# DeltaNet heads of a decoder layer, taken in pairs through one chain of steps instead of singly through two alternating chains

## The chip, the cores and the metric

One core of one Trainium2 chip runs the whole program. The metric is device time in microseconds (us), as the median of several runs; lower is better. The engines are named as the profile names them: PE is TensorE (matmuls), PEld its load of weights, DVE is VectorE, ACT is ScalarE, POOL is GpSimd, and SP issues most transfers.

## What is computed

One layer of a hybrid decoder, for a prompt of 512 tokens and for 8 sequences of 4 sample tokens, which share the weights. Width is 1024, all in float32. The layer is a half-step feed-forward, a token mixer, and a second half-step feed-forward. The mixer has one large input projection and two branches, whose gated outputs are added and projected again. Branch A is a gated DeltaNet with 8 heads of 128 by 128, branch B a sliding-window attention. Cut to the mixer and the delta rule:

```python
proj = h @ p['w_in']
u, z, b_raw, a_raw, q_sw, k_sw, v_sw, gate_a, gate_b = jnp.split(proj, split_idx, axis=-1)
u, conv_new = short_conv(u, conv_buf, p['conv_w'])
...
o_dn, S_new = gated_delta_rule(q_dn, k_dn, v_dn, g, beta, S0)
o_dn = rmsnorm(o_dn, p['dn_norm']) * jax.nn.silu(z)
...
y = jax.nn.sigmoid(gate_a) * o_dn + jax.nn.sigmoid(gate_b) * o_sw
return y @ p['w_out'], ...

def gated_delta_rule(q, k, v, g, beta, S0):
    # S_t = a_t (I - b_t k_t k_t^T) S_{t-1} + b_t k_t v_t^T,  o_t = S_t^T q_t
    ...
    lower = jnp.where(strict, einsum('bnhid,bnhjd->bnhij', kb, kc) * decay, 0.0)
    sol = triangular_solve(eye(C) + lower, rhs)
    ...
    def step(S, xs):
        v_new = un - wn @ S
        o = (qn * exp(gn)) @ S + an @ v_new
        S = S * exp(g_last) + k_dec.T @ v_new
        return S, o
```

For the prompt the kernel uses chunks of 128 tokens, so a head has 4 chunks (`NC`). For each it inverts a triangular 128 by 128 matrix; then the state S goes through the chunks one after the other.

## The kernel before

**Products.** Each float32 weight and activation is split into a high and a low part of the type fp32r (hi and lo of a weight; hh and hl of an activation), and a product is three matmuls: hi with hh, hi with hl, lo with hh. They are the matmuls of line L301, on 272 columns (half of the 544 tokens). The split of a weight is one pass on ACT (L270, hi) and one on DVE or POOL (L271, lo).

**The mixer's work, and who orders it.** The instructions' order is found on the host by `Streams` (L145 to L181). A main stream gives units of projections to TensorE in the order of `ORDER` (L49): the blocks B, U0 and U1 (the columns of q, k and v of heads 0 to 3), K, V and Q of the attention, then U2, G0, U3 and G1 to G7 (G is a gate block: a gate of the attention, z and a gate of the DeltaNet, one block for each head). Side streams (the DeltaNet chains, the attention, the sample tokens' DeltaNet, the merges) are generators. At each `yield` they give a cost, which moves a virtual clock on, and a delay, times `LATK`, after which they are due again; whenever a unit of the main stream has been put in, the streams that are due put in their next step. The side streams' steps thus stand between projections. When main has no more units ahead of a wait, the side streams' steps follow one another.

**The DeltaNet chains.** Two streams run `delta_stream` (`NSTR` = 2): one takes the heads 0, 2, 4, 6, the other 1, 3, 5, 7. Each takes one head at a time (`G` = 1), so the tiles of a chain hold M = G x NC = 4 matrices. The chain of a head, in `delta` and `inverse`:
- E from memory (L1249), the decays Dm (L1252 and the exps on ACT), transposes pkt of k (L1260) with squares on ACT, and the rsqrt rk: 11 small DVE instructions in a row (L340 to L345).
- pkq (L1281), NT and AT on DVE (L1285, L1287).
- `inverse`: the 32 by 32 diagonal blocks of NT go to memory and back (L1393, L1398), which puts the 16 by 16 blocks one to a partition. Then come 15 steps of two DVE instructions, a product pr (L1420) and a subtraction (L1422), then a way back through memory (L1427, L1430), and four levels of small matmuls (L1440, L1448 and L1451, L1464, L1474 and L1478, L1486, L1491), each with a copy or subtraction on ACT or DVE.
- transposes (L1301), kdec and vs (L1302) and the scaling of k and q (L1304) on DVE.
- the loop over the chunks: pks (L1317), R on DVE (L1319), pvn (L1325), vn on ACT (L1328), psu (L1333) and poT (L1339, L1341), the state S on DVE (L1344, in the first chunk the copy L1348), od and the square o2 on ACT (L1350, L1352), the sum tq on POOL (L1354).
- at the head's end pro (L1362), rx (L1364), the rsqrt ro, prb (L353, called at L1369), the product od on DVE (L1370), and the store of od to memory (L1372).

`merge_stream` loads a head's od again (L1540) when both od and the gate z (L1526) of that head are there, and merges them (L1547, L1549). At the mixer's end main waits for the merges of the heads 0 to 3, splits them into hh and hl, gives TensorE the first halves of two blocks of the output projection (w_out), then does the same for the heads 4 to 7 (L1909 to L1917). The chain's last results are therefore needed by the second halves of these two blocks and by all that follows.

Of the kernel before, what the change touches and what calls it, by code (L numbers as in the profile page):

```python
# [28 lines left out]
FF = 2752  # L29
NH = 8  # L30
NC = SEQ // P
G = 1
NSTR = 2
M = G * NC
EPS = 1e-6
NEG = -1e30
# [29 lines left out]
WD = 0  # L66
HP_S = 300
HP_E = 0
KQ_BUFS = 4
L_CVO = 2.0  # L70
L_B1 = 6.0
L_SUB = 3.5
# [715 lines left out]
class Mixer:  # L788
# [431 lines left out]
    def head_blocks(self, gi):  # L1220
# [3 lines left out]
        def tiles():  # L1224
            if not st:
                st["kq"] = self.kqp.tile([P, G, 2, SEQ], F32, tag="kq", name="kq")
                st["v"] = self.kqp.tile([P, G, SEQ], F32, tag="vT", name="vT")
            return st["kq"], st["v"]

        for n in range(G):  # L1230
            h = gi * G + n
            for kind, outs in ((1, lambda n=n, h=h: (tiles()[0][:, n, 0, :], self.kqs[:, h, 0, :])),
                               (0, lambda n=n, h=h: (tiles()[0][:, n, 1, :], self.kqs[:, h, 1, :])),
                               (2, lambda n=n, h=h: (tiles()[1][:, n, :], self.vts[:, h, :]))):
                use = self.conv_block(kind, h, outs)
                if n == G - 1 and kind == 2:
                    def use(ps, f=use):
                        f(ps)
                        self.kqv[gi] = tiles()
# [136 lines left out]
    def delta_stream(self, i, dp):  # L1376
        for gi in range(i, NH // G, NSTR):
            while gi not in self.kqv or not self.decays_done:
                yield 0.0, 1.0
            yield from self.delta(gi, *self.kqv[gi], dp, i)  # L1380
# [311 lines left out]
    def run(self, sch, feed):  # L1692
# [5 lines left out]
        c_ap, c_rp, c_tp, c_sp = ExitStack(), ExitStack(), ExitStack(), ExitStack()  # L1698
        self.kqp = L.pool("kqp", KQ_BUFS, ctx)
        self.cvp = L.pool("cvp", 1, ctx)  # L1700
        self.sc = {}
        self.conv_load(0)
        self.gp = L.pool("gp", 1, ctx)
        dps = [L.pool(f"dp{i}", 1, ctx) for i in range(NSTR)]
        self.ap = L.pool("ap", 1, c_ap)
# [46 lines left out]
    def plan(self, feed):  # L1752

        L, win, x = self.L, self.win, self.x
        self.att_done = [0] * 4
        self.kqv, self.z, self.gb_done = {}, [None] * NH, [False] * NH
        self.od_done, self.merged = [False] * NH, [False] * 10
        self.decays_done = False
        self.odd = L.dr.tile([NH, P, SEQ], F32, name="odd")
        qT, kT = (lambda: self.qT), (lambda: self.kT)  # L1760
        q = lambda c: [u for b in range(8) for u in L.project(win, Q0 + b * P, x, self.evac(qT, b, (c,)), cs=(c,),
                                                              pool_lo=False)]
        self.mark0 = feed.add(q(0))
        self.marks = []

        def ba(ps):
            self.sch.spawn(self.decays(ps, self.rp), 0)

        for n in ORDER:
            if n == "B":  # L1770
                us = L.project(win, BA0, x, ba, ncol=16)
            elif n == "Q":
                us = q(1)
            elif n == "K":
                us = [u for b in range(2) for u in L.project(win, K0 + b * P, x, self.evac(kT, b))]
            elif n == "V":
                us = [u for b in range(2) for u in L.project(win, V0 + b * P, x, self.v_block(b))]
            elif n[0] == "U":
                us = [u for h in (0, 1) for u in self.head_blocks(2 * int(n[1]) + h)]
            else:  # L1780
                us = self.gate_blocks(int(n[1]))
            self.marks.append((n, feed.add(us)))
# [186 lines left out]
```

## Time and profile before

| | |
|---|---|
| median of 3 runs | 1608.23 us (1606.12 to 1611.68) |
| the profiled execution | 1608.77 us |
| its span, first to last instruction | 1607.0 us |
| mean granted TensorE clock | 0.983 of full speed |
| the mixer's DeltaNet | about 550 to 1130 us of the span |
| busy: PE, DVE, ACT, POOL | 96%, 55%, 40%, 19% of the span |

The span is shorter than the execution's time by what lies around the first and the last instruction. The two levels of TensorE's clock are 1.2 and 2.4 GHz, so a granted clock of 0.90 in a stretch means that it ran at the lower one for a fifth of it. Matmuls are pipelined, and a busy TensorE isn't one at its peak. The busy shares are averages over stages that differ; the windows show the stages.

### The profile page before, as it was taken

What the parts mean: (1) busy time and instruction counts of PE and PEld (TensorE: products, weight loads), DVE (VectorE), ACT (ScalarE), POOL (GpSimd) and SP (SyncE); (2) the same over time, 40 slices, a digit from 0 to 9 for tenths busy, and PEclk for the clock granted to TensorE, in tenths of its full rate; (3) what the DMA queues carried; (4) which work ended last, traced back from release to release, by engine and by line L of the source; (5) the groups of instructions that cost most, each with busy time, mean ns of one, the idle gap of its engine ahead of it and who ended that gap; (6) DMA issues with size and microseconds to landing.
All of it is one profiled execution on the core that took longest, in us unless ns stands there. A gap on an engine that the chain in (4) does not pass through costs nothing.

```text
span 1607.0 us, 33057 instructions
## 1 busy us (share of the span) xinstructions
PE 1537.5 (96%) x12851; PEld 1418.5 (88%) x12851; DVE 887.6 (55%) x2384; ACT 640.1 (40%) x1449; POOL 305.9 (19%) x443
## 2 busy tenths in 40 slices
PE   7999999999998999998999999999979999999996
PEld 4799999999977999997778888889979999999995
DVE  5433322333598787688889568665474332233365
ACT  4322222222445544445575242223556332223363
POOL 2000000000343231231122134131458000000042
PEclk9999999999999999999999899999999999999998
DMA  9554445445655334653113243624515432333353
GB/s 314 169 183 138 153 136 159 147 148 153 190 167 178 100 75 107 165 135 77 45 45 80 77 121 83 167 55 130 158 53 158 115 86 87 94 87 89 83 152 111
DMA packets 316083, 199.69 MB, mean 124 GB/s; under 512 B 37508, under 2 KB 298335, under 8 KB 315638
## 3 DMA queue, kind: packets, MB, share of 16 engines
q1 hardware_dynamic: 315638, 197.46, 43.5%
q8 instruction: 101, 1.65, 0.4%
q14 instruction: 56, 0.46, 0.1%
q0 software_dynamic: 288, 0.11, 0.0%
HBM read 182.08 MB, written 16.36 MB: 123 GB/s over the span
## 4 chain that ended last, share of the span: by engine, by line
PE 77%; DVE 13%; ACT 3%; DMA 2%; issue 2%; POOL 2%; SPq 0%; DVEq 0%; ACTq 0%; POOLq 0%
PE pg L301 16%; PE pu L301 16%; PE pb L301 16%; PE pd L301 14%; PE adaps L467 3%; DVE y L1194 2%; DVE lo L271 2%; ACT hi L270 1%; PE pov L1065 1%; DVE X L1422 1%; PE pgu L301 1%; DVE s L1016 1%; PE psc L1012 1%; PE pkq L1281 1%; DVE xT L571 1%
## 5 line engine op out<-in xcount | busy, mean ns | idle before, releaser
L270 ACT CAST hi<-raw 128x512 fp32r<-128x512 f32 (+2 forms) x502 | 287.9, 581 | 613.1 <-PE pu L301 172.1
L271 DVE TENSOR_TENSOR lo<-raw,hi 128x512 fp32r<-128x512 f32 (+2 forms) x368 | 252.9, 688 | 385.8 <-ACT hi L270 378.7
L301 PE MATMUL pb<-hh,hi 128*128 128x272 f32 (+1 forms) x1008 | 234.9, 303 | 1.4 <-ACT hi L270 0.7
L271 POOL TENSOR_TENSOR lo<-raw,hi 128x512 fp32r<-128x512 f32 (+1 forms) x104 | 140.6, 1356 | 483.1 <-ACT hi L270 460.5
L301 PE MATMUL pb<-hh,lo 128*128 128x272 f32 (+1 forms) x1008 | 227.7, 296 | 1.3 <-POOL lo L271 0.7
L301 PE MATMUL pb<-hl,hi 128*128 128x272 f32 (+1 forms) x1008 | 227.2, 295 | 1.0 <-DVE hl L271 1.0
L301 PEld LDWEIGHTS pb<-hh,hi 128*128 128x128 f32 (+1 forms) x1008 | 164.6, 191 | 12.0 <-issue 6.5
L301 PE MATMUL pd<-fh,hi 128*128 128x272 f32 x704 | 171.3, 290 | 0.0
L301 PE MATMUL pd<-fl,hi 128*128 128x272 f32 x704 | 170.2, 289 | 0.0
L301 PEld LDWEIGHTS pb<-hl,hi 128*128 128x128 f32 (+1 forms) x1008 | 165.0, 190 | 3.6 <-DVE hl L271 1.5
L301 PEld LDWEIGHTS pb<-hh,lo 128*128 128x128 f32 (+1 forms) x1008 | 164.4, 191 | 4.1 <-DVE lo L271 1.4
L301 PE MATMUL pd<-fh,lo 128*128 128x272 f32 x672 | 162.4, 289 | 4.0 <-POOL lo L271 2.2
L301 PE MATMUL pg<-hh,hi 128*128 128x272 f32 x672 | 149.6, 292 | 7.5 <-ACT hh L538 3.6
L301 PE MATMUL pu<-hh,hi 128*128 128x272 f32 x672 | 148.2, 291 | 0.0
L301 PE MATMUL pg<-hl,hi 128*128 128x272 f32 x672 | 147.0, 289 | 0.3 <-DVE hl L539 0.2
L301 PE MATMUL pu<-hl,hi 128*128 128x272 f32 x672 | 146.1, 289 | 0.0
L301 PE MATMUL pu<-hh,lo 128*128 128x272 f32 x672 | 145.3, 288 | 0.7 <-POOL lo L271 0.7
L301 PE MATMUL pg<-hh,lo 128*128 128x272 f32 x672 | 145.6, 288 | 0.0
L301 PEld LDWEIGHTS pd<-fh,hi 128*128 128x128 f32 x704 | 119.9, 188 | 8.6 <-issue 4.2
L301 PEld LDWEIGHTS pg<-hh,hi 128*128 128x128 f32 x672 | 108.8, 189 | 19.6 <-ACT hh L550 5.0
L301 PEld LDWEIGHTS pd<-fl,hi 128*128 128x128 f32 x704 | 120.2, 188 | 0.0
L301 PEld LDWEIGHTS pd<-fh,lo 128*128 128x128 f32 x672 | 114.1, 188 | 5.6 <-POOL lo L271 2.9
(469 smaller groups left out, 2628.6 us busy)
## 6 DMA issues: line engine op xcount, KB each, us to landing
raw<-w_in SPq DMA_DIRECT2D x136, 256.0 KB, 3.2
wa<-w_ada SPq DMA_DIRECT2D x56, 512.0 KB, 4.4
raw<-ffn_w_gate SPq DMA_DIRECT2D x94, 256.0 KB, 2.9
raw<-ffn_w_up SPq DMA_DIRECT2D x94, 256.0 KB, 7.0
raw<-ffn_w_down SPq DMA_DIRECT2D x92, 256.0 KB, 3.0
wb<-w_ada SPq DMA_DIRECT2D x32, 256.0 KB, 5.8
S<-state_delta SPq DMA_DIRECT2D x8, 512.0 KB, 8.0
delta_sample<-S SPq DMA_DIRECT2D x8, 512.0 KB, 3.4
```

The source lines that it names most:

```text
L270: self.nc.scalar.copy(out=hi, in_=raw)
L271: (eng or self.nc.vector).tensor_tensor(out=lo, in0=raw, in1=hi.bitcast(F32), op=ALU.subtract)
L301: self.nc.tensor.matmul(out=ps[:m, c, :TH], lhsT=a[:r, kt, :m], rhs=b[:r, kx, c * TH:(c + 1) * TH], start=first and i == 0, stop=last and ...
L467: self.ada_mm = nc.tensor.matmul(out=ps[32 * j:32 * j + 32, :], lhsT=self.cT[:, k, :], rhs=was[j], start=k == 0, stop=k == 7, skip_group_c ...
L571: nc.vector.tensor_tensor(out=self.xT[:, b, s], in0=self.xT[:, b, s], in1=t[:, :n], op=ALU.add)
L1012: nc.tensor.matmul(out=ps[:, i * 256:i * 256 + nk], lhsT=self.qT[64 * h:64 * h + 64, 2 * g + i, qb * P:(qb + 1) * P], rhs=self.kd[64 * h:6 ...
L1016: nc.vector.tensor_tensor_reduce(out=s[:, i, :nk], in0=ps[:, i * 256:i * 256 + nk], in1=am[:, lo:], scale=0.125, scalar=-3e38, op0=ALU.add ...
L1065: nc.tensor.matmul(out=po[64 * h:64 * h + 64, :256], lhsT=self.vn[:, c, 64 * g:64 * g + 64], rhs=pTs[kb][:, 2 * h:2 * h + 2, :], start=kb ...
L1194: nc.vector.scalar_tensor_tensor(out=y[:, :CVN], in0=cv[:, i:i + CVN], scalar=w[i], in1=y[:, :CVN], op0=ALU.mult, op1=ALU.add)
L1281: nc.tensor.matmul(out=pv[:, j], lhsT=kq[:, n, 0, c * P:(c + 1) * P], rhs=kq[:, n, :, c * P:(c + 1) * P], start=True, stop=True)
L1422: e.tensor_tensor(out=xs, in0=xs, in1=pv, op=ALU.subtract)
```

## The change

`G` goes from 1 to 2 and `NSTR` from 2 to 1. One stream takes four pairs of heads, (0, 1) to (6, 7), and every tile of the chain holds M = 8 matrices. `KQ_BUFS`, the buffers for k, q and v, go from 4 of one head to 2 of a pair, which is the same space. The list of the units of a U block is written for the new numbering, and its units stay the same.

```diff
-G = 1
-NSTR = 2
+G = 2
+NSTR = 1
 M = G * NC
...
-KQ_BUFS = 4
+KQ_BUFS = 2
...
             elif n[0] == "U":
-                us = [u for h in (0, 1) for u in self.head_blocks(2 * int(n[1]) + h)]
+                us = self.head_blocks(int(n[1]))
```

What a step covers follows from the shapes in `delta` and `inverse`. Operations on whole tiles (Dm's sum, R, od, o2, tq, all of `inverse`, the rsqrts) become one instruction with twice the elements, or on twice the partitions; loops over heads or matrices (`for n in range(G)`, `for m in range(M)`: the matmuls, vn, S, kdec, vs, the exps) have the same instructions in all, two heads' in a row. The program has 11440 PE instructions before and after; DVE has 2386 before and 2082 after, ACT 1353 and 1301, POOL 448 and 400, SP 879 and 822.

The steps of the inverse on DVE, before; X is the tile of 16 by 16 blocks, the L1194 rows are the convolution of the next heads:

```order
L1420 TENSOR_TENSOR pr<-X_8472,B 32x64
L1422 TENSOR_TENSOR X_8472<-X_8472,pr 32x8x8
L1420 TENSOR_TENSOR pr<-X_8472,B 32x63
L1422 TENSOR_TENSOR X_8472<-X_8472,pr 32x9x7
L1194 SCALAR_TENSOR_TENSOR y<-cv,cwT,y 128x600
```

and the same steps of the second pair after:

```order
L1420 TENSOR_TENSOR pr<-X_8732,B 64x64
L1016 ISA s,mx<-psc,cst 128x256
L1016 ISA mx 128x1
L1422 TENSOR_TENSOR X_8732<-X_8732,pr 64x8x8
L1057 COPY pT<-ppt 128x512
L1420 TENSOR_TENSOR pr<-X_8732,B 64x63
```

The same number of elements stands in each partition, on 64 partitions instead of 32, and there are half as many such steps in the program; here rows of the attention (L1016, L1057) stand between them.

The last head's chunks on PE, before (the L301 rows are projections, the L1661 rows the sample tokens' DeltaNet):

```order
L1317 MATMUL pks<-S,kq 128x128
L1661 MATMUL psu_14048<-vm,skdec 128x512
L1661 MATMUL psu_14051<-vm,skdec 128x512
L1325 MATMUL pvn<-R,X 128x128
L301 MATMUL pb<-hh,hi 128x272 x2
L301 MATMUL pb<-hl,hi 128x272 x2
L301 MATMUL pb<-hh,lo 128x272 x2
L301 MATMUL pb<-hh,hi 128x272 x2
L301 MATMUL pb<-hl,hi 128x272 x2
L301 MATMUL pb<-hh,lo 128x272 x2
L1333 MATMUL psu<-vn,kdec 128x128
L1339 MATMUL poT<-kq,S 128x128
```

and the last pair's after, down to the first projection behind it:

```order
L1317 MATMUL pks<-S,kq 128x128 x2
L1325 MATMUL pvn<-R,X 128x128 x2
L1333 MATMUL psu<-vn,kdec 128x128
L1339 MATMUL poT<-kq,S 128x128
L1333 MATMUL psu<-vn,kdec 128x128
L1341 MATMUL poT<-AT,vn 128x128
L1339 MATMUL poT<-kq,S 128x128
L1341 MATMUL poT<-AT,vn 128x128
L1362 MATMUL pro<-ones,tq 128x64 x8
L353 MATMUL prb<-ident,ro0y 128x128 x8
L301 MATMUL pb<-hh,hi 128x272 x3
```

Before, 12 projection matmuls stand between a chunk's steps. Now the chunks 1 to 3 of the last pair, pro and prb follow one another with no other matmul between them; from the last matmuls of the inverse (L1491) to prb there are 12 projection matmuls in all. The first projection after prb belongs to the second halves of the output projection's first two blocks. On SP the last pair's order is the two stores odd, then the two loads odm. On DVE it is the merge of head 6 and its hl, the merge of head 7, three splits of weights of the output projection, and head 7's hl.

## Rows read from the trace of the kernel before

**Rows 1.** Page, part 1: busy time, share of the span, instructions.

```profile
PE 1537.5 (96%) x12851; PEld 1418.5 (88%) x12851; DVE 887.6 (55%) x2384; ACT 640.1 (40%) x1449; POOL 305.9 (19%) x443
```

**Rows 2.** Windows over the mixer: us; busy PE, PEld, DVE, ACT, POOL; PEclk, DMA share, GB/s.

```profile
550.00:700.00 150.00, 145.60 (x1349) 139.88 (x1348) 113.55 (x320) 73.19 (x172) 39.15 (x93) 1.00 0.47 116
700.00:900.00 200.00, 188.00 (x1761) 158.92 (x1760) 172.57 (x684) 111.18 (x336) 39.47 (x92) 0.96 0.30 73
900.00:1130.00 230.00, 222.97 (x2224) 201.49 (x2222) 153.11 (x473) 74.67 (x195) 60.85 (x73) 0.96 0.41 109
```

**Rows 3.** Windows: the mixer's worst 50 us, and a stretch of the first feed-forward.

```profile
700.00:750.00 50.00, 42.00 (x289) 38.31 (x290) 45.17 (x149) 22.61 (x56) 14.70 (x34) 0.90 0.47 109
...
300.00:400.00 100.00, 100.00 (x791) 93.08 (x790) 32.48 (x54) 28.47 (x48) 0.00 (x0) 1.00 0.52 154
```

**Rows 4.** Waits of PE, 450 to 1130 us: total us, times, longest us.

```profile
PE ppt L1051 <- issue: 6.1, 1, 6.1
...
PE prb L353 <- DVE ro1y L345: 2.0, 2, 1.9
...
PE pb L301 <- DVE hl L271: 1.0, 2, 0.6
```

**Rows 5.** Groups of DVE, 550 to 1130 us: count | busy us, mean ns | idle before.

```profile
L1422 DVE TENSOR_TENSOR X<-X,pr 32x15 f32<-32x15 f32 (+7 forms) x120 | 27.2, 229 | 1.5
L1420 DVE TENSOR_TENSOR pr<-X,B 32x15 f32<-32x15 f32 (+7 forms) x120 | 25.1, 211 | 1.4
...
L1304 DVE TENSOR_TENSOR kq<-kq,E 128x1024 f32<-128x1024 f32 x8 | 10.2, 1280 | 0.0
...
L1319 DVE TENSOR_TENSOR R<-vs,pks 128x128 f32<-128x128 f32 x24 | 6.8, 284 | 4.5 <-PE pks L1317 4.2
...
L1287 DVE TENSOR_TENSOR AT<-pkq,Dm 128x256 f32<-128x256 f32 x16 | 6.5, 409 | 0.0
...
L1302 DVE TENSOR_TENSOR kdec<-pkt,edec 128x512 f32<-128x512 f32 x8 | 5.5, 686 | 0.8 <-PE pkt L1301 0.7
```

**Rows 6.** Timeline of the last chunk before: start us, us, what [idle before].

```profile
1088.76 0.38 PE L1317 MATMUL pks<-S,kq 128*128 128x128 f32 x2
...
1089.18 0.29 DVE L1319 TENSOR_TENSOR R<-vs,pks 128x128 f32<-128x128 f32 x1 [0.19 <-PE pks L1317]
...
1090.98 0.49 PE L1325 MATMUL pvn<-R,X 128*128 128x128 f32 x2
...
1091.57 0.37 ACT L1328 ACTIVATE vn<-pvn,b 128x128 f32<-128x128 f32 x1 [3.67 <-PE pvn L1325]
...
1092.81 0.38 PE L1333 MATMUL psu<-vn,kdec 128*128 128x128 f32 x2
...
1093.03 0.39 PE L1339 MATMUL poT<-kq,S 128*128 128x128 f32 x2
...
1093.46 0.35 DVE L1344 SCALAR_TENSOR_TENSOR S<-S,eg,psu 128x128 f32<-128x128 f32 x1 [1.68 <-PE poT L1339]
...
1094.76 0.46 POOL L1354 TENSOR_TENSOR tq<-tq,o 128x128 f32<-128x128 f32 x1
...
1098.59 1.00 PE L1362 MATMUL pro<-ones,tq 128*128 128x64 f32 x8
```

**Rows 7.** Timeline of head 6's rsqrt: rx and the last of its 11 instructions.

```profile
1080.08 0.16 DVE L1364 TENSOR_SCALAR rx<-pro 128x4 f32<-128x4 f32 x1 [0.55 <-PE pro L1362]
...
1083.09 0.16 DVE L345 SCALAR_TENSOR_TENSOR ro0y<-ro0a,ro0y 128x4 f32<-128x4 f32 x1
```

**Rows 8.** DMA issues: queue, operation, count, KB each, median us from issue to landing.

```profile
odd<-od SPq DMA_DIRECT2D x8, 256.0 KB, 2.7
odm<-odd SPq DMA_DIRECT2D x8, 256.0 KB, 2.8
```

**Rows 9.** Timeline of the mixer's end: the last store of od, the last z.

```profile
1107.68 0.34 SPq L1372 DMA_DIRECT2D odd<-od  x1
...
1119.56 0.72 DVE L1526 SCALAR_TENSOR_TENSOR z<-tg,z 128x544 f32<-128x544 f32 x1
```

## The prediction, before the change was run

> **What bounds the kernel now.** I read the page's busy times first. TensorE is busy for 1537.5 of 1607.0 us, VectorE for 887.6 [rows 1]. Read over the whole span that says TensorE alone counts; the stretches say where it doesn't. Next came the windows over the mixer [rows 2], the only part that the change touches. TensorE is idle for 4.4, 12.0 and 7.0 us in the three stretches, 23.4 in all, and the granted clock is 1.00, 0.96 and 0.96. At 0.96 the chip gives away 8.0 us of the 200 and 9.2 us of the 230, together 17.2. VectorE is busy 172.6 of 200 us in the middle stretch, where TensorE idles most. In the worst 50 us TensorE is idle for 8.0 us and the clock is 0.90, 5 us lost, while in a stretch of feed-forward it is busy 100.00 of 100 at clock 1.00 [rows 3]: idle time and lowered clock stand together. The view of TensorE's waits [rows 4] names one long one, 6.1 us before the transposes ppt, put down to issue; the tile they read is scaled on VectorE (L1042). It also has 2.0 us for the rsqrt's result ro1y, and 1.0 at the end of the mixer. Everything else of TensorE's time is matmuls, whose number doesn't change. So up to 23.4 + 17.2 = 40.6 us lie in reach of any change to the chains, no more, and what a chain leaves bare at its end is lost on top.
>
> The end of the mixer was read row by row [rows 9]. A merge takes a head's od and the gate tile z. The last head's od is sent to memory at 1107.68, and the last z is begun only at 1119.56. The chain is 12 us early, so TensorE doesn't wait for it there.
>
> **The change, part by part.** *VectorE gets less work.* The 15 steps of the inverse run on 64 partitions instead of 32, with as many elements in each. Of 240 instructions 120 remain. They took 27.2 + 25.1 = 52.3 us [rows 5]; half, 26.1, goes. The rsqrts of a chain (11 instructions, L340 to L345) run 8 times instead of 16, on 8 columns instead of 4: 88 instructions less at 0.16 us [rows 7] are 14. VectorE has 304 fewer instructions in all by the order, so 96 others go, each joined to its pair. One with 128 elements takes 284 ns (R), one with 256 takes 409 (AT) [rows 5]; joining two saves 2 x 284 - 409 = 159 ns, so 96 save about 15, an estimate. In all some 55 of the mixer's 439 us, in the middle stretch an eighth of 172.6, about 21.
>
> What that is worth lies between nothing (TensorE waits only where the waits name VectorE, and what replaces these waits is the pair's longer step) and the 40.6 above. I tie it to the middle stretch, the only one with VectorE scarce: 12.0 idle plus 8.0 of clock are 20, and I take four fifths: **-16**.
>
> *The steps of the chain get longer.* Each covers two heads, and there is no second chain to put beside it. Where projections lie between the steps this costs nothing: they cover it at 126 ns a matmul (791 in 100 us) [rows 3]. The order shows that they do so for the first three pairs, but not for the last. Before, the last chain is spread over the last gate units, with 12 projection matmuls between two steps. Now its last chunks, pro and prb stand back to back, and behind them come only the output projection's units, which read the merges of heads 6 and 7. Their cover is gone. I build that piece from rows:
> - After the inverse's last product: 1.2 us for its matmuls to drain (an estimate), the copy X (0.41, as AT), then for each head kdec, vs and kq, 0.69 + 0.68 + 1.28 [rows 5], so 5.3 for two (vs taken as kdec); with the first chunk's start 7.9.
> - A chunk, from rows 6: pks to R 0.42; R with two heads 0.41 (as AT); pvn to vn 0.59; vn twice, 0.37 each; psu to S 0.65; S twice, 0.35 each; with issue between them some 0.3. Together 3.8. Chunks 1 to 3: 11.5. That makes 19.4.
> - The sum on POOL ends 1.4 after S (1095.22 against 1093.81), 1.7 with the second head; pro 1.0 and 0.4 to hand over [rows 6]; rx with the rsqrt, 1080.08 to 1083.25 [rows 7], 3.2: 25.7. prb 1.2 and two products od at 0.69 (512 columns, as kdec): 28.3.
> - The store odd 2.7 and the load odm 2.8 [rows 8]; the load for head 6 stands behind both stores on SP: 33.9 with issue.
> - A merge is two operations on 512 columns, then come hh on ACT and hl on VectorE; at kdec's 0.69 each, head 6's product can begin near 36, head 7's last part near 41, as three splits of weights stand ahead of hl.
>
> So TensorE has 41 us. In these it has 60 matmuls of the chain at 0.22 (psu's start to poT's) and 8 of pro in 1.0, 12 projection matmuls, 1.5, and 2 us of head 6's product: 18. **Idle +23** [rows 6]. Bounds: 13 if the steps overlap as well as in one chain (chunks at 2.9, splits early, loads cheap), 30 if every hand-over is 0.3 longer. Just ahead, the inverse's last levels have 2 to 4 matmuls between them where a level waits about half a microsecond for VectorE or ACT: **+2** (0 to 5). The 1.0 of before for hl [rows 4] is in the new wait: **-1**.
>
> *The clock.* After TensorE's idle 8.0 us the granted clock was 0.90 over 50 us [rows 3], 5 us lost; in feed-forward nothing. A new idle 23 us in pieces should cost something of that size: nothing to 7, and I take **+3**.
>
> *Neither.* ACT's exps, squares and copies and POOL's memsets (both under half busy [rows 2]) hide as before; the inverse's DMAs number half as many at double size, and SP's loads of weights run ahead of use.
>
> Sum: -16 + 23 + 2 - 1 + 3 = +11 on the profiled 1608.8 (span 1607.0 and 1.8 around it; the runs' median is 0.5 lower): 1619.8, forecast **1620**. Own range: 1608 to 1638, by tail 13 to 30, relief 6 to 20 and clock, not all at their ends at once.
>
> **A rule weighed.** Rows 5 give a saving of 159 ns for each joined instruction, whatever TensorE does meanwhile. The Trainium skill (Perfetto Trace Analysis, Optimizing Scalar/DVE Operations) says grouping raises throughput where the engine is saturated, but that breaking instructions up may finish work sooner where it isn't and still leaves bubbles on other engines. By its first half alone the sum would be the relief without the tail, some 1593; by the second alone the tail without the relief, 1636. The rows show each in its own stretch: VectorE at 86% in 700 to 900, and TensorE with nothing but the chain at the end.
>
> **Rivals.**
> 1. *VectorE sets TensorE's pace through the whole mixer (faster).* Then its 55 us bring 30 of the 40.6, the tail is at its short end (13) and the clock costs 1: -30 + 13 + 1 (levels, hl) + 1 = -15, **1594**. It decides from a relief of about 26. For it: 86% busy, the 6.1 us wait at VectorE's densest place, the clock below 1.00. Against: the named waits on VectorE are a few us, and the first stretch has VectorE at 76% with TensorE idle for only 4.4.
> 2. *Both balance, or TensorE's work is all that counts.* A relief of 25 meets a tail of 24: **1608**. The matmuls are 11440 instructions in both orders, and TensorE is 96% busy. The Trainium skill (Perfetto Trace Analysis, Identifying the Most-Contended Engine) would have the most-contended engine optimized first; that engine's work is unchanged here, so by it nothing moves.
> 3. *The chain is late for every pair.* Projections between steps were placed for delays that the doubled steps exceed, so a pair's four chunks also stall TensorE by 2 us each for three pairs, 24, and there is little relief: 11 + 24 + 6 = +41, **1650**.
> That the change does nothing is excluded by the order's counts.
>
> **How the numbers follow.** Forecast 0.5, rival 1 0.2, rival 2 0.2, rival 3 0.1. A difference under 0.3% (4.8 us) can hardly be told from none, so "same" is 1603.4 to 1613.0. Faster: rival 1 and a sliver of rival 2, 0.22. Same: most of rival 2, and the forecast's low end, 0.22. Slower: the rest, 0.56. The range takes in the forecast and rival 2 whole, half of rival 1 and none of rival 3's upper half: **1594 to 1641**.
>
> **What would show it.** In the changed profile: VectorE near 833 us busy; in the middle stretch TensorE's idle below 5 us and the clock near 1.00; at the mixer's end a stretch of about 40 us with TensorE half idle, waits of pks for S and of vn, psu, prb and of the output projection's hh and hl, and the clock lowered there or just behind. The last merge should wait for od's load, not for z. Wrong would be a chain that ends ahead of z, a tail under 12 us idle, or stalls of the same size at the earlier pairs.

## The result, and the profile after

The changed kernel takes 1619.05 us (median of 12 runs, 1615.71 to 1624.38) beside 1608.24 for the kernel before (12 runs). The ratio is 1.007, with an interval from 1.0055 to 1.0084: slower, by about 11 us. The forecast was 1620. The profiled execution of the change is one of its longer ones, 1623.84 us with a span of 1622.0 and a mean granted clock of 0.973.

The page's busy times, which answer to [rows 1]:

```profile
PE 1535.5 (95%) x12851; PEld 1418.7 (87%) x12851; DVE 859.1 (53%) x2080; ACT 633.5 (39%) x1397; POOL 293.0 (18%) x395
```

VectorE is busy 28.5 us less. The windows over the mixer, which answer to [rows 2], and behind them its last 39 us, the 14 us at the end of these, and a stretch that is spoken of last (us; busy PE, PEld, DVE, ACT, POOL; PEclk, DMA share, GB/s):

```profile
550.00:700.00 150.00, 146.99 (x1330) 142.19 (x1329) 98.01 (x212) 63.49 (x134) 35.06 (x76) 0.95 0.47 119
700.00:900.00 200.00, 186.98 (x1725) 161.04 (x1724) 163.19 (x572) 117.76 (x347) 38.59 (x81) 0.97 0.29 73
900.00:1130.00 230.00, 214.79 (x2284) 192.83 (x2282) 143.49 (x379) 65.81 (x159) 53.26 (x55) 0.97 0.37 100
...
1103.00:1142.00 39.00, 21.16 (x135) 18.09 (x133) 17.97 (x41) 8.51 (x22) 3.50 (x5) 0.80 0.11 33
1128.00:1142.00 14.00, 4.08 (x17) 3.32 (x15) 7.03 (x11) 3.37 (x6) 0.60 (x1) 0.50 0.26 81
...
660.00:690.00 30.00, 29.33 (x216) 27.63 (x215) 14.03 (x23) 9.73 (x19) 5.57 (x11) 0.80 0.45 114
```

In 700 to 900 VectorE has 9 us less to do, and TensorE's idle time didn't fall: 13.0 us, where it was 12.0. At the mixer's end TensorE is idle 17.8 of 39 us, and in the last 14 of these its clock is at half. The timeline of that stretch shows the last pair's chunks, 3.9 to 4.05 us apart, then the wait for the rsqrt, the way through memory, and the two waits for hh:

```profile
1109.29 0.71 PE L1317 MATMUL pks<-S,kq 128*128 128x128 f32 x4 [0.16 <-DVE S L1348]
...
1113.19 0.87 PE L1317 MATMUL pks<-S,kq 128*128 128x128 f32 x4
1114.57 0.71 PE L1325 MATMUL pvn<-R,X 128*128 128x128 f32 x4 [0.51 <-DVE R L1319]
1115.80 0.49 PE L1333 MATMUL psu<-vn,kdec 128*128 128x128 f32 x2 [0.52 <-ACT vn L1328]
...
1117.24 0.87 PE L1317 MATMUL pks<-S,kq 128*128 128x128 f32 x4
...
1123.00 1.33 PE L1362 MATMUL pro<-ones,tq 128*128 128x64 f32 x10 [0.93 <-POOL tq L1354]
1126.81 1.97 PE L353 MATMUL prb<-ident,ro0y 128*128 128x128 f32 x8 [2.48 <-DVE ro0y L345]
...
1128.74 1.12 SPq L1372 DMA_DIRECT2D odd<-od  x2
1130.83 4.29 SPq L1540 DMA_DIRECT2D odm<-odd  x2
1133.31 0.75 DVE L1547 SCALAR_TENSOR_TENSOR odm<-odm,cwT,z 128x512 f32<-128x512 f32 x1 [3.81 <-DMA odm<-odd]
...
1135.51 1.05 PE L301 MATMUL pb<-hh,hi 128*128 128x272 f32 x3 [6.74 <-ACT hh L270]
...
1137.46 0.75 DVE L1547 SCALAR_TENSOR_TENSOR odm<-odm,cwT,z 128x512 f32<-128x512 f32 x1 [1.24 <-DMA odm<-odd]
...
1141.87 0.59 PE L301 MATMUL pb<-hh,hi 128*128 128x272 f32 x1 [3.19 <-ACT hh L270]
...
1143.40 0.82 PE L301 MATMUL pb<-hl,hi 128*128 128x272 f32 x2 [0.27 <-DVE hl L271]
```

The waits of TensorE from 1103 to 1145 (total us, times, longest) come to 18.1 us. The first line alone is more than half:

```profile
PE pb L301 <- ACT hh L270: 9.9, 2, 6.7
PE prb L353 <- DVE ro0y L345: 2.5, 1, 2.5
PE psu L1333 <- ACT vn L1328: 2.0, 4, 0.5
PE pvn L1325 <- DVE R L1319: 1.5, 3, 0.5
```

The last merge (1137.46) waits for od's load and not for z, the other way round than in [rows 9].

### The profile page after: what moved, and what is told of

It reads as the page before. It is cut to its first block, busy times and chain, and to the rows that moved or that the text cites. A ratio compares the mean times of both kernels' runs of the same rounds, so it can differ in the third digit from the quotient of the medians.

```text
span 1622.0 us, 32557 instructions
## 1 busy us (share of the span) xinstructions
PE 1535.5 (95%) x12851; PEld 1418.7 (87%) x12851; DVE 859.1 (53%) x2080; ACT 633.5 (39%) x1397; POOL 293.0 (18%) x395
## 4 chain that ended last, share of the span: by engine, by line
PE 80%; DVE 11%; ACT 3%; DMA 3%; issue 2%; POOL 1%; SPq 0%; DVEq 0%; ACTq 0%; POOLq 0%
PE pb L301 18%; PE pg L301 16%; PE pu L301 16%; PE pd L301 14%; PE adaps L467 3%; DVE y L1194 2%; DVE lo L271 1%; PE psu L1661 1%; PE pkq L1281 1%; PE pgu L301 1%; DVE xT L571 1%; DMA raw<-ffn_w_down 1%; ACT hi L270 1%; DVE s L1016 1%; PE ppt L1051 1%
## 5 line engine op out<-in xcount | busy, mean ns | idle before, releaser
L301 PE MATMUL pb<-hh,hi 128*128 128x272 f32 (+1 forms) x1008 | 235.9, 304 | 10.3 <-ACT hh L270 9.9
L301 PE MATMUL pb<-hl,hi 128*128 128x272 f32 (+1 forms) x1008 | 226.5, 295 | 0.3 <-DVE hl L271 0.3
L301 PE MATMUL pb<-hh,lo 128*128 128x272 f32 (+1 forms) x1008 | 226.1, 295 | 0.2
L301 PEld LDWEIGHTS pb<-hh,hi 128*128 128x128 f32 (+1 forms) x1008 | 165.8, 192 | 22.1 <-ACT hh L270 10.6
L301 PE MATMUL pd<-fh,hi 128*128 128x272 f32 x704 | 171.4, 290 | 0.0
L301 PE MATMUL pd<-fl,hi 128*128 128x272 f32 x704 | 170.1, 289 | 0.0
L301 PEld LDWEIGHTS pb<-hl,hi 128*128 128x128 f32 (+1 forms) x1008 | 165.8, 192 | 2.6 <-issue 0.7
L301 PEld LDWEIGHTS pb<-hh,lo 128*128 128x128 f32 (+1 forms) x1008 | 165.2, 192 | 2.8 <-issue 0.9
L301 PE MATMUL pd<-fh,lo 128*128 128x272 f32 x672 | 162.3, 289 | 4.7 <-DVE lo L271 2.7
L301 PE MATMUL pg<-hh,hi 128*128 128x272 f32 x672 | 150.0, 293 | 7.3 <-ACT hh L538 3.6
L301 PE MATMUL pu<-hh,hi 128*128 128x272 f32 x672 | 148.8, 292 | 0.0
L301 PE MATMUL pg<-hl,hi 128*128 128x272 f32 x672 | 147.1, 290 | 0.2 <-DVE hl L539 0.2
L301 PE MATMUL pu<-hl,hi 128*128 128x272 f32 x672 | 146.6, 289 | 0.0
L301 PE MATMUL pu<-hh,lo 128*128 128x272 f32 x672 | 145.7, 288 | 0.7 <-POOL lo L271 0.7
L301 PE MATMUL pg<-hh,lo 128*128 128x272 f32 x672 | 145.8, 289 | 0.0
L301 PEld LDWEIGHTS pd<-fh,hi 128*128 128x128 f32 x704 | 119.9, 188 | 8.8 <-issue 4.2
L301 PEld LDWEIGHTS pg<-hh,hi 128*128 128x128 f32 x672 | 109.1, 190 | 19.9 <-issue 5.0
L301 PEld LDWEIGHTS pd<-fl,hi 128*128 128x128 f32 x704 | 120.2, 188 | 0.0
L301 PEld LDWEIGHTS pd<-fh,lo 128*128 128x128 f32 x672 | 114.1, 188 | 6.2 <-DVE lo L271 3.6
```

Source lines behind the costliest of these rows:

```text
L301: self.nc.tensor.matmul(out=ps[:m, c, :TH], lhsT=a[:r, kt, :m], rhs=b[:r, kx, c * TH:(c + 1) * TH], start=first and i == 0, stop=last and ...
```

## The experiments

**Theories.** T: the loss is the last pair's bare end, and what the pairing does elsewhere is a gain smaller than that. R1: the doubled steps are late for every pair. R2: VectorE's relief is large, and the end is larger still. C and D (what VectorE's work in the chain is worth) and K (TensorE's clock) came up on the way. Times are medians; "before" beside a run is the kernel before on the same chip.

**1. All delays of the chain at five sixths** (`a_dn83`).

```diff
-L_DN = 0.9
-L_INV = 1.0
+L_DN = 0.75
+L_INV = 0.833
...
-L_B1 = 6.0
-L_SUB = 3.5
+L_B1 = 5
+L_SUB = 2.92
...
-L_BNC = 13.0
+L_BNC = 10.8
```

> The changed kernel with the delays of the DeltaNet chain's steps, which set how many projections stand between two steps, cut to five sixths. The last pair's prb then stands at projection matmul 5960 of 9520 (6104 in the change, 5936 before the change), so its chunks have projections between them again. Theory T (the loss is the bare end of the last chain, about 20 us; VectorE's relief gives some 8 back): about 1600 us, 1596 to 1605. Rival R1 (the doubled steps come late for every pair, the end is only one of four such places): steps closer together stall TensorE more often, 1619 to 1630. Rival R2 (the relief is worth 16 or more, and the end costs 27): 1592 or below.

1605.97 us beside 1608.57 (ratio 0.9981, 0.9959 to 1.0002). R1's time and R2's 1592 are missed. T has the direction; the time is 1 us outside its range. Experiment 8 shows how far this edit can be trusted.

**2. The inverse's steps split again** (`a_split`).

```diff
-            pv = box(pr, 0, (w, n), (1, w))
-            xs = box(X16, j + 1, (16, n), (1, w))
+            for r, _ in halves:
+                pv = box(pr[r], 0, (w, n), (1, w))
+                xs = box(X16[r], j + 1, (16, n), (1, w))
...
```

> The changed kernel with the 15 steps of the inverse done on the two halves of 32 partitions one after the other: 240 DVE instructions again instead of 120, 26 us more VectorE work, all else as in the change. T (relief worth about 8 us for 55 us of VectorE work): +4, about 1623. R2 (16 or more for 55): +8 or more, 1627 and above. If VectorE's load doesn't matter at all: 1619.

1647.97 us (ratio 1.0257, 1.0233 to 1.0281), 29 more than the change, for 28 us more VectorE work (page: 886.9 us busy, 859.1 in the change). R2's bound is met, but 29 is far over what a relief of 16 for 55 us gives (8), and about as much as the added work itself. The end isn't what grew: TensorE is idle there for 17.7 us, as in the change, and its other idle time between the 3600th and the 6300th projection matmul is 37.8 us where the change has 22.6. The added steps stand in the chain itself, so VectorE's load and a longer chain aren't told apart.

**3. The kernel before with half of the inverse's steps** (`b_half`).

```diff
-            pv = box(pr, 0, (w, n), (1, w))
-            xs = box(X16, j + 1, (16, n), (1, w))
+            if j % 2:
+                pv = box(pr, 0, (w, n), (1, w))
+                xs = box(X16, j + 1, (16, n), (1, w))
...
```

> The kernel before with 8 of the 15 steps of the inverse left out (the even ones), so 128 of 240 DVE instructions and about 28 us of VectorE work less, in the old order; part of the inverse isn't computed. T: -4, about 1604. R2: -8 or more, 1600 or below. If VectorE's load doesn't matter: 1608.

1605.94 us (ratio 0.9994, 0.9981 to 1.0008): no gain that can be told from none, for 15 us less of VectorE's busy time (page: 872.4). R2 falls, and T's -4 doesn't show either: taking VectorE work away doesn't speed up the old order.

**4. The last pair's od merged in place** (`a_direct`).

```diff
-            nc.sync.dma_start(out=self.odd[h], in_=od[:, n, :])
+            if gi == NH // G - 1:
+                self.od_sb[h] = od[:, n, :]
+            else:
+                nc.sync.dma_start(out=self.odd[h], in_=od[:, n, :])
```

and the merge takes `od_sb[b]` in place of a load where it is there.

> The changed kernel with the last pair's od merged where it lies, without the store to memory and the load back. In the change's trace the load for head 6 landed 4.6 us after its store was issued, and head 7's 8.7 us after. T: these lie bare at the end, so -5 to -8, about 1612. R1: the end isn't what costs, within 2 us of 1619.

1611.56 us, 7.5 below the change (ratio to before 1.0015, 0.9995 to 1.0036). T as forecast. In its timeline the projection waits half as long for hh:

```profile
1114.24 1.19 PE L353 MATMUL prb<-ident,ro0y 128*128 128x128 f32 x8 [2.48 <-DVE ro0y L345]
...
1118.94 1.05 PE L301 MATMUL pb<-hh,hi 128*128 128x272 f32 x3 [3.51 <-ACT hh L270]
```

**5. The change with half of the inverse's steps** (`a_half`; the edit of 3).

> The changed kernel with 8 of the 15 steps of the inverse left out (the even ones), so 56 of 120 DVE instructions and about 14 us of VectorE work less; part of the inverse isn't computed. Theory C (VectorE's work in the pair's single chain counts nearly in full, as the 26 us added by splitting cost 29): -10 or more, 1609 or below. Theory D (VectorE's limit is one-sided: more of it costs, less of it gives little, as in the kernel before): within 4 us of 1619.

1624.09 us (1614.27 to 1626.45; ratio 1.0098, 1.008 to 1.0116), 5 above the change. The edit takes out 64 instructions, not 56, and 11 us of VectorE's busy time (page: 848.2). C falls; D's band is missed by 1 us, on the slow side. Less VectorE work brings nothing in the new order either.

**6. The kernel before with each product of the inverse done twice** (`b_more`).

```diff
-            e.tensor_tensor(out=pv, in0=box(X16, j, (16, n), (0, w)), in1=box(B, 17 * j + 1, (0, n), (1, w)),
-                            op=ALU.mult)
+            for _ in range(2):
+                e.tensor_tensor(out=pv, in0=box(X16, j, (16, n), (0, w)), in1=box(B, 17 * j + 1, (0, n), (1, w)),
+                                op=ALU.mult)
```

> The kernel before with the product of each of the inverse's 15 steps done twice: 120 DVE instructions and about 25 us of VectorE work more, in the old order, the result the same. C (two alternating chains cover each other's VectorE work): +3 to +10, at most 1618. D (VectorE is as scarce in both): +25, about 1633.

1621.57 us (ratio 1.0081, 1.0066 to 1.0096): +13, between the two, for 19 us more of VectorE's busy time (page: 906.9, and 887.6 before). Work added to VectorE costs in both orders, about 0.7 us for each us here and 1.0 in the pairs' single chain (experiment 2); work taken away gives nothing that shows in either.

**7. All delays at three quarters** (`a_dn75`; the edit of 1).

> The changed kernel with the delays of the DeltaNet chain's steps cut to three quarters: the last pair's prb stands at projection matmul 5804, 156 further ahead than with five sixths. T (only the bare end costs, and five sixths already hid it): the same as that, about 1606. If steps that stand closer together cost by themselves: 1609 or above. If five sixths left part of the end bare: 1602 or below.

1624.86 us (ratio 1.0099, 1.0082 to 1.0116), 19 above experiment 1, though its end is covered as well, so T's forecast fails. The mean granted clock over its runs is 0.967, where experiment 1 has 0.976. As (1 - clock) times the span that is 53.6 us lost against 38.5, which is 15 of the 19. What lowers the clock there is not shown.

**8. The kernel before with five sixths** (`b_dn83`; the edit of 1).

> The kernel before with the same delays at five sixths, as a control: its chains end ahead of the last gate already. T: nothing to hide, within 4 us of 1608. If shorter delays help a chain whatever its end: 1603 or below, and then part of what they gave the change isn't the end. If they hurt by themselves: 1613 or above.

1623.95 us (ratio 1.0091, 1.0073 to 1.011): shorter delays hurt the old order. So they aren't good in themselves, and experiments 1 and 7, which move every step, measure the end only within some 15 us.

**9. Shorter delays for the last two pairs alone** (`a_from2_6`). This leaves the order as it is in the change up to the third pair.

```diff
-            yield from self.delta(gi, *self.kqv[gi], dp, i)
+            f = 0.6 if gi >= 2 else 1.0
+            for cost, lat in self.delta(gi, *self.kqv[gi], dp, i):
+                yield cost, f * lat
```

> The changed kernel with the delays of the chain's steps cut to 0.6 for the last two pairs alone: the order is the change's up to the third pair, and the last prb stands at projection matmul 5954 instead of 6104. Theory T (the bare end costs): 1601 to 1608. Theory K (a good part of the loss is TensorE's clock, which in the change's trace falls behind the pairs' blocks of 32 by 32 matmuls in the inverse, wherever the chain ends): faster than 1619, but the mean granted clock stays under 0.978, where the kernel before has 0.982. R1 (closer steps stall TensorE): 1619 or above.

1597.33 us beside 1608.31 (ratio 0.9932, 0.991 to 0.9953). Against the change's 1.007 that is 1.4%, 22 us, for covering the end: more than T expected. K's sign is missing: the mean clock over the runs is 0.982. Its last prb ends at 1091, ahead of the last z, and the last merge follows z at once, as before the change (this kernel's lines from L1381 on stand two further down):

```profile
1089.99 1.04 PE L353 MATMUL prb<-ident,ro0y 128*128 128x128 f32 x8
...
1104.33 0.72 DVE L1528 SCALAR_TENSOR_TENSOR z<-tg,z 128x544 f32<-128x544 f32 x1
1105.09 0.78 DVE L1549 SCALAR_TENSOR_TENSOR odm<-odm,cwT,z 128x512 f32<-128x512 f32 x1
```

Its windows over the times at which the change had its bare end, and over 660 to 690 (columns as above):

```profile
1100.00:1140.00 40.00, 38.68 (x301) 37.81 (x301) 18.42 (x39) 21.70 (x44) 14.70 (x15) 1.00 0.60 188
...
660.00:690.00 30.00, 29.33 (x213) 27.73 (x212) 14.05 (x23) 9.72 (x19) 5.56 (x11) 0.78 0.46 109
```

TensorE is idle for 1.3 us there in place of 17.8, at the full clock. The work at these times isn't the same; between the 6092nd and the 6120th projection matmul, where the change waits, TensorE is idle for 17.8 us in the change, 0.6 in this run and 0.6 before.

**10 and 11. The inverse's levels cut into pieces** (`a_spr70`, `a_spr65`).

```diff
         for m in range(M):
+            if m and m % NC == 0:
+                yield 0.25, SPR
```

and the like between the pieces of the next two levels; the delays of 1 at 0.7 and at 0.65.

> The changed kernel with the levels of the pair's inverse cut into pieces of 8 to 16 small matmuls with a yield between them, so that projections can stand there (they do for the first, third and last pair), and with the delays at 0.7, so that the last prb stands at 5925, as far ahead of the end as before the change. K (the dense small matmuls lower the clock): mean granted clock 0.980 or above over the runs, against 0.976 with five sixths of the delays and 0.967 with three quarters, and 1592 to 1602 us. If the clock falls for another reason: 0.976 or below, 1604 or above. If the extra hand-overs cost more than the clock gives: clock 0.980, but 1606 or above.

> The same with the delays at 0.65: the last prb at 5828, and the pieces fall at other places between the projections. K and a time that doesn't hang on the accidents of one order: within 4 us of the run with 0.7, clock 0.980 or above. If such accidents decide: more than 6 us from it, to either side.

1605.99 us (ratio 0.9986, 0.9973 to 0.9999) at a mean clock of 0.979, and 1607.8 (0.9998, 0.9983 to 1.0014) at 0.982. The clock rises over experiments 1 and 7, and the time stays 4 us and more above K's range. The two runs lie 2 us apart, so these two orders agree. Since delays and pieces were changed together, what the pieces do by themselves stays open.

**12. The last two pairs at 0.7** (`a_from2_7`).

> As with 0.6 for the last two pairs' delays, but 0.7: the last prb at projection matmul 6008, between that run's 5954 and the change's 6104; some 90 projection matmuls, 12 us, still stand behind it. T (it is the end's cover that counts, not the accidents of one order): 1595 to 1604, within 4 us of the run with 0.6 but for what of the merges' way through memory lies bare. If accidents of an order decide, as the whole-chain runs with five sixths and three quarters suggest (1606 and 1625): more than 6 us from the run with 0.6.

1602.17 us beside 1609.14 (ratio 0.9958, 0.9944 to 0.9973): inside T's range, 5 us above experiment 9, so neither its 4 us nor the rival's 6 decides. A second order with most of the end covered, and the change's order ahead of it, is faster than the kernel before as well.

## Why the prediction was right, point by point

**The end was right; that the sum came within 1 us is partly luck.** The prediction set -16 for what pairing gives in the middle against +27 for the end (+23 idle, +2, -1, +3 of clock). Experiment 9 separates them as far as one order can, since it has the pairs and a covered end: 0.9932 against before is -11 us for the pairs, and the 1.4% from there to the change are +22 for the end. Both terms were about 5 us too large, and the errors cancelled. The mechanism of the +27 held. That of the -16 didn't, and the 11 us came another way (below). Of the signs that the prediction named, those at the end came; in the middle VectorE is at 859 us and not 833, the idle time at 13.0 and not below 5.

**The end, step by step.** The prediction's 41 us from the inverse's last product to head 7's last part, behind hl, are 40 in the timeline (1103 to 1143.40), and head 6's product begins after 33, not 36. Its chunks of 3.8 are 3.9 to 4.05, and pro to prb is 3.8 where the sum has 4.6, set by the rsqrt as said. TensorE's idle time is 17.8 us where 23 were expected: the 18 us of work in it took 21.16, part of them at the lower clock. Store and load were put at 5.5 with issue on top and measured 4.6 from odd's issue to the first merge; taking both away gave 7.5 (experiment 4), since head 7's load lay bare too: its merge begins 4.15 us behind head 6's. The clock's +3 is of the right size: 0.80 over 39 us are 7.8 us lost, but mostly in idle time. Laid over the busy time of TensorE, the trace's stretches of lowered clock cost 2.6 us up to 1142 and 2.2 more in the 5 us behind:

```profile
1142.00:1147.00 5.00, 4.73 (x20) 4.30 (x21) 3.02 (x4) 2.90 (x7) 0.77 (x1) 0.53 0.99 301
```

With the idle 17.8 that makes 22.6 us, counted in the change's trace alone, beside the 22 that experiment 9 won back.

**VectorE's relief was over-sized, and its mechanism failed.** The inverse's instructions went from 25.1 + 27.2 [rows 5] to 14.1 + 12.9 us, as predicted:

```profile
L1420 DVE TENSOR_TENSOR pr<-X,B 64x15 f32<-64x15 f32 (+7 forms) x60 | 14.1, 236 | 2.5 <-DMA B<-nd 1.2
L1422 DVE TENSOR_TENSOR X<-X,pr 64x15 f32<-64x15 f32 (+7 forms) x60 | 12.9, 216 | 1.3
```

The whole saving is 28.5 us of busy time, half of the 55 that were summed from single durations. The durations did fall by 47 us, from 992.7 to 945.5 in all; but they overlap in the trace (the 992.7 are 887.6 us of busy time), so one that goes frees less than its length. The step that failed is the next one, that it would end TensorE's idle time and lowered clock between 700 and 900: 12.0 us idle became 13.0. The 6.1 us wait of [rows 4] is gone, but others stand in its place, by these rows of the change's waits in 700 to 900:

```profile
PE ppt L1051 <- ACT s L1039: 2.4, 3, 0.9
PE pkc L1091 <- DMA kc<-cache_swa_k: 2.0, 1, 2.0
PE psp L1126 <- DVE sc L1119: 1.4, 1, 1.4
```

Experiments 3 and 5 say the same: less work on VectorE alone gives nothing. A smaller misreading changed nothing: ACT isn't under half busy throughout, as the prediction says, but at 111.18 of 200 us in the middle stretch [rows 2]. The Trainium skill (Perfetto Trace Analysis, Optimizing Scalar/DVE Operations) says that grouping can raise throughput if the engine is saturated, and that breaking up instructions may let work finish sooner where the engine isn't and still leaves bubbles on others. VectorE's busy time here agrees with the first half, the kernel's time doesn't show it; the second half no run tested at the end.

**Where the pairs' 11 us come from** is seen by comparing stretches of equal progress: from the 3600th to the 6300th of the 9520 projection matmuls. The windows of the kernel before, the change, and experiment 9, one fence each:

```profile
559.80:1155.10 595.30, 571.70 (x5445) 515.22 (x5444) 436.27 (x1470) 265.08 (x709) 148.08 (x260) 0.97 0.40 103
```

```profile
560.90:1168.80 607.90, 567.53 (x5449) 513.97 (x5448) 410.30 (x1173) 259.37 (x665) 137.00 (x216) 0.96 0.38 100
```

```profile
560.30:1139.90 579.60, 558.75 (x5449) 507.33 (x5448) 404.59 (x1173) 259.52 (x665) 131.94 (x216) 0.98 0.40 105
```

TensorE's idle time is 23.6, 40.4 and 20.9 us. The change against before has 16.8 us more of it, about the 17.8 of its end; outside the end it has 22.6. Experiment 9 has 2.7 us less idle time than before, but 13 us less busy time for the same matmuls, about a third of that through the clock (0.98 against 0.97 in these two executions). Over all runs the clock is the same in both (0.982), so the gain of 11 us is mostly busy time at a given clock.

The other traces bear this out. TensorE's busy time in this stretch, less what the lowered clock took of it, is the matmuls' own time:

| traces | matmuls' own time |
|---|---|
| two chains: before, experiments 3, 6, 8 | 555.5, and 554 to 561 |
| pairs: the change, experiments 9, 1, 2, 4, 5, 7, 12 | 546.0, 547.1, and 544 to 549 |
| pairs with the inverse's levels cut: experiments 10, 11 | 552 and 553 |

So the pairs with whole levels take some 8 us less of TensorE's own time, whatever the delays and whatever VectorE has to do. Here the prediction's other premise failed: it left TensorE's work as it was because the number of matmuls is. What in the pairs' order makes the same matmuls shorter stays open. The number of changes from a projection to a matmul of the chain doesn't sort the orders: 106 before and 77 in the change, but 93 in experiment 9 and 94 in 10 and 11. That long rows of the chain's matmuls are what counts, which cutting the levels undoes, would fit; no run shows it alone.

**The rivals.** The first (VectorE sets the pace, 1594) is out by the result and by experiments 3 and 5. The third (late for every pair, 1650) is out by the result and by the idle time outside the end, 22.6 us beside 23.6 before. The second, that only TensorE's work counts and nothing moves, is out by the result's interval and by experiment 9.

## What to carry to other kernels

Joining two alternating chains into one of doubled steps costs where a chain ends with nothing left to put beside it, so follow the last chain in the new order down to who needs it: building that piece instruction by instruction from rows of the old trace gave its length within 2 us, and its parts within 4. Don't take busy time freed, summed from durations, for time gained. Then move the end rather than undo the change. Here shorter delays for the last two pairs turned 1.007 into 0.9932 of the kernel before, the fastest of the versions run. Test such a move with everything ahead of it unchanged; runs that moved every step scattered by 15 us and more.

## What was not expected

**The clock also falls where TensorE waits little.** The prediction tied it to idle time. Between 640 and 660 TensorE works through the small matmuls of the first pair's inverse (L1440 to L1478), which now come for two heads at once, with projections between them. TensorE's instructions there have the same order in the change and in experiments 9 and 4. These are their windows, one fence each:

```profile
640.00:660.00 20.00, 18.71 (x343) 17.37 (x342) 8.08 (x18) 6.47 (x15) 2.75 (x3) 0.96 0.75 185
```

```profile
640.00:660.00 20.00, 19.47 (x344) 17.83 (x343) 7.46 (x17) 6.16 (x13) 2.74 (x3) 0.90 0.77 191
```

```profile
640.00:660.00 20.00, 19.14 (x367) 17.35 (x365) 7.67 (x17) 6.00 (x13) 2.87 (x4) 1.00 0.73 178
660.00:690.00 30.00, 29.84 (x244) 29.09 (x245) 18.06 (x32) 12.92 (x28) 7.86 (x16) 1.00 0.59 153
```

In the first two the clock falls to its lower level before 660 and stays there for part of 660 to 690 (0.80 and 0.78, shown above); in the third it keeps the higher level. TensorE was idle for 1.3, 0.5 and 0.9 us ahead of it, so idle time alone doesn't separate them. The same instructions are granted different clocks in different executions, and what decides isn't shown. Within the change's 12 runs the mean clock goes from 0.970 (1624.38 us) to 0.977 (1615.71 us), which is enough for their scatter of 9 us: 0.007 of the span is 11 us. The median clock is 0.975 where before has 0.982, 11 us more lost, 7 of them in the last 14 us of the bare end, much of which was idle anyway.

**VectorE's work is worth different amounts upward and downward.** By the pages, 19 us more cost 13 in the old order and 28 us more cost 29 in the new; 15 us less in the old order gave at most 3, not to be told from none, and 11 us less in the new gave nothing. A place that seems to have slack by one test may have none by the other.
